# The keys of an RWKV mixer: two-part products in the dense projections, or exact float32 products among the scan's steps

## The chip, the cores and the metric

One core of a Trainium2 chip. The metric is the device time of one execution in microseconds (us). The kernel before was timed three times: 2986.07, 2990.43 and 2999.31 us; the median, 2990.43, stands for it.

## The reference

A stack of four layers of a model with 1024 features, batch 1: a short convolution and an attention layer (with feed-forward and mixture of experts) on 256 tokens, then two layers on 256 latent and 256 context tokens. The last layer's mixer is RWKV, and the change lies in it alone. Cut to what matters:

```python
def rwkv_project(h, shifted, mu, w_rkv, w0, w1, w2, a0, a1, a2, g1, g2, kvec):
    xx = shifted - h
    xr, xw, xk, xv, xa, xg = (h + xx * mu[i] for i in range(6))
    r = xr @ w_rkv[0]
    k = xk @ w_rkv[1]
    v = xv @ w_rkv[2]
    ...
    kk = to_heads(k * kvec[0], RW_HEADS).astype(jnp.float32)
    kk = kk / jnp.maximum(jnp.sqrt(jnp.sum(kk * kk, axis=-1, keepdims=True)), 1e-12)
    k = k * (1 + (a - 1) * kvec[1])

def rwkv7_scan(r, w, k, v, kk, a, S):
    def step(S, inp):
        rt, wt, kt, vt, kkt, at = inp
        sa = jnp.einsum("bhvk,bhk->bhv", S, -kkt)
        S = S * wt[:, :, None, :] + sa[..., None] * (kkt * at)[:, :, None, :] + vt[..., None] * kt[:, :, None, :]
        return S, jnp.einsum("bhvk,bhk->bhv", S, rt)
```

The keys `k` are one product: 512 tokens (context and latent) by 1024 features, with a 1024x1024 weight. Everything is float32.

## The kernel before

**Two ways to multiply float32.** Most dense products are made of two parts in the type float32r: `wchunk` (L254, L255) loads a 512 KB chunk of weights, ScalarE copies it into a high part `whi`, VectorE subtracts that to get the low part `wlo`; the other operand is split in the same way, and three products (high x high, high x low, low x high) are summed. `gemmN` (its products are L293) does this for features on partitions, a pair of 128-column blocks at a time. An exact product of plain float32 operands is one instruction in the program and two rows (passes) in the trace.

**Projections, `rwkv_project`.** `mix(i)` makes one of the six mixes of h and its shift, block by block of 128 features, and splits it into `mh` and `ml` (9 buffers each). First come the values V (L1591), 192 products of 128x512. Then `lowrank` (L1576) makes the first halves of the decay (`th`, 24 products of 128x512), of the in-context rate (`am`, 24 of 64x512), and of the gate (`gm`, 24 of 128x256). The keys' operand `kS` is left as plain float32: eight VectorE instructions, after `am`. The receptance's operand `rS` is made likewise. The residual x is then spilled to memory (`xd`, 1 MB), since its tile is used for the keys' weights and results.

**Scan, `rwkv_scan`.** The 1024 features are eight blocks of 128 (two heads each); a block b and a sequence s (0 context, 1 latent) are a unit, 16 in all. Each unit has stages, written as Python generators: `early` (decays, normalised keys kk, operands of the chunks; kk's last instruction is L1784), `inverse1`, `inverse2` (L1945 with the operand XX), `start_rh`, `chain` (four chunks of 64 tokens; L2015, L2022, L2027, L2038, L2045), `finish` and `finish2` (head norm, bonus, gate: L2078, L2095, L2097, L2103). A scheduler at the end of `rwkv_scan` takes, time and again, the generator with the earliest due time (the table PACE, in halves of a block's period) and runs it up to its next yield; so the order of instructions on every engine is fixed when the program is built. `receptance` (L1733) is one more generator at the start, and `project_a` to `project_7` make the output projection at the end.

**Keys in the scan.** `key_pieces` makes a block's keys in 16 exact products of 128x256 (L1698), each a piece of its own, into a PSUM bank named `kc`, and a ScalarE copy (L1703) into the second half of x's tile; the weights come in four DMAs of 128 KB into its first half. The pieces are drawn in order: 16 by a generator `k0` and 32 by `k1` at the scan's start, and 80 in the chains: by the table KP each chunk of units 0 to 9 issues one piece ahead of L2027 and one ahead of L2038:

```python
    KP = ((0, 1, 1),) * 10 + ((0, 0, 0),) * 6
    K0T = ((0.0, 0.02), (0.3, 0.08))
    NDS = ((0, 0, 0),) * 10 + ((2, 3, 3),) * 5 + ((0, 0, 0),)
...
        gens.append([K0T[0][0], K0T[0][1], keys(16, 1), "k0", []])
        gens.append([K0T[1][0], K0T[1][1], keys(32, 3), "k1", ["k0"]])
```

The first `early` waits for `k0`, the second block's for `k1`. By the table NDS the chains of units 10 to 14 issue products of zeros instead (L1994, bf16: 2, 3 and 3 for each chunk), which fill the array between small products.

Of the kernel before, what the change touches and what calls it, by code (L numbers as in the profile page):

```python
# [10 lines left out]
I32 = mybir.dt.int32  # L11
# [21 lines left out]
def _body(es, tc, A, out, upto, dbg):  # L33
# [10 lines left out]
    class Psum:  # L44
        def tile(self, shape, dtype, name, bufs=None, tag=None):
            tag = tag or name
            tag = sizes.get(tag) if isinstance(sizes.get(tag), str) else tag     # one tag may stand for another
            return self.pool.tile(shape, dtype, name=name, tag=tag, bufs=sizes.get(tag, 1))
# [3 lines left out]
    def phase(nm, banks, raw=4, hl=3, work=True, t2=6, sq2=2):  # L52
        """buffers of a phase: psum banks by tag, streamed weights, small temporaries"""
# [37 lines left out]
    def columns(name, parts):  # L91
        """parts: list of (key, AP [n,128]) with at most 128 rows; loads them -> function that gives {key: [128, n]}"""
# [35 lines left out]
    # silu(c) in zeros, to be placed at any column of 32; and silu(c_2), silu(c_ctx_2) side by side  # L128
# [4 lines left out]
    # [p, m]: 1 where p % 32 == m  # L133
# [6 lines left out]
    back.update(jobs=[], rate=0.0, credit=0.0)  # L140

    def back_step():
        """one step of the first job; clean: it holds no buffer now"""
        while back["jobs"]:
            try:
                back["clean"] = next(back["jobs"][0])
                return
            except StopIteration:
                back["jobs"].pop(0)

    def background(jobs, chunks):
        """add jobs (steps, generator), to be done within so many chunks"""
# [9 lines left out]
    def mods(name, W, n0, ncols, strip, nv, bcols):  # L162
        """W [1024, N]: columns n0..n0+ncols of silu(c) @ W + b -> one [128, ncols/128] per vector, (steps, generator)
        strip 0: for c; 1: for c_2 (and c_ctx_2). Four column groups of the array share the blocks of 128 rows;
        each run of 512 columns has its rows (one per vector) among the 32 of a group"""
# [32 lines left out]
    def mods_v(name, W, n0, ncols, vecs, bcols):  # L198
        """the same by VectorE: the sums over blocks of 128 rows, then over partitions"""
# [39 lines left out]
    def wchunk(ap, shape):  # L239
        """ap (or a list of APs side by side in the last dim), [128, a, b] with a * b <= 1024"""  # L240
# [17 lines left out]
    def gemmA(W, cols, xh, xl, emit, kmax=4):  # L258
        """feature-major: for each list of 128-column blocks (pairs) emit(pair index, psum [128,2,256])
        cols: list of lists of column starts handled in one chunk (2 blocks each)"""  # L260
# [15 lines left out]
    def gemmN(W, cols, xs, emit):  # L276
        """feature-major; xs: (hi, lo) [128, n] per block of features; emit(block, psum [128, n])"""
# [26 lines left out]
    lnw = const.tile([P, 1], F32, name="lnw")  # L304

    def warm_ln(after):
        """have the logarithm's table loaded once `after` is there, ahead of a norm"""
# [4 lines left out]
    class Stats:  # L312
        """sum over features of x^2, block by block of 128 as x comes to be; rstd: 1/sqrt(mean + eps), the same in all 128 rows.
        vec: VectorE adds the blocks up, else TensorE"""
# [40 lines left out]
    def modulated(pl, x, a, b, tag="h", bufs=3, st=None):  # L355
        """rms-normalised x times column a plus column b, in two parts"""
# [15 lines left out]
    def rstd2(x):  # L372
        """for x [128, 8, 2, 256]"""
# [5 lines left out]
    def scale_col(name, g, s):  # L379
        """g * (1 + s)"""  # L380
# [4 lines left out]
    def load_T(src, x):  # L385
        """[256, 1024] -> x [128, 8, 256]; loads, -> function that transposes"""
# [16 lines left out]
    xj = act.tile([P, KT, 2, T], F32, name="xj")     # residual streams: context, latent  # L403
# [85 lines left out]
    def layer1_attn():  # L489
# [7 lines left out]
        # rope tables, tokens on partitions  # L497
# [25 lines left out]
        # additive masks [query, tile's keys]: query tile 0 sees keys 0..127, query tile 1 keys 0..255  # L523
# [19 lines left out]
        # a group's heads i, 5 + i, 10 + i have one softmax: the groups' weights by their sums make it so  # L543
# [5 lines left out]
        def scores(i):  # L549
            """scores, masked; exp of them less their maximum; over their sum"""  # L550
# [61 lines left out]
        # probabilities, transposed; outputs feature-major  # L612
        oh = fb.tile([P, 8, T], F32R, name="oh", tag="h", bufs=3)
        ol = fb.tile([P, 8, T], F32R, name="ol", tag="h", bufs=3)
        for b in range(8):
# [4 lines left out]
            for h in range(2 * b, min(2 * b + 2, NH)):  # L620
                r0 = 64 * (h % 2)
                pt = ps.tile([P, 512], F32, name="tr", bufs=2)
                # [keys 0..127 | q tile 0, q tile 1], [keys 128..255 | q tile 1]
# [47 lines left out]
    def layer1_moe():  # L671
# [22 lines left out]
        # tokens on partitions, two parts  # L694
# [36 lines left out]
        # place of each token among its expert's tokens  # L731
# [99 lines left out]
        # an expert with more than 128 tokens: its other tokens  # L831
# [11 lines left out]
    def columns2():  # L843
        """loads; -> function that makes the columns"""
# [36 lines left out]
    def masks0(pl):  # L881
        nonlocal capf, capb, glm, reset, mdir, ones8
        # masks over pairs of tokens in one 128-token tile, [s, t]
# [6 lines left out]
        # t - s within chunks of 64, s on partitions twice  # L890
# [6 lines left out]
        # 0 where a chunk of 64 starts (forwards, backwards)  # L897
# [5 lines left out]
        mdir = pl.tile([8, 2], F32, name="mdir")     # 1 for forward rows, 1 for backward rows  # L903
# [4 lines left out]
    # states handed from the context scans to the latent scans  # L908
# [1429 lines left out]
```

## Time and profile before

| | us |
|---|---|
| runs of the kernel before | 2986.07, 2990.43, 2999.31 |
| their median | 2990.43 |
| the profiled execution, its span (no other time is given for it) | 2995.0 |
| TensorE products busy | 2811.6 (94%) |
| TensorE weight loads busy | 2282.7 (76%) |
| VectorE busy | 2269.9 (76%) |
| ScalarE busy | 1739.7 (58%) |
| share of the span of TensorE in the chain that ended last | 42% |

The span is that of one profiled execution; times of rows count from its start. PE is TensorE and PEld its weight loads, DVE VectorE, ACT ScalarE, POOL GpSimd, SP SyncE, which issues the DMAs. The end of a product is modelled (products overlap), so the distance of two starts says what one costs, and its busy time is longer. The RWKV projections end at 2224.25 us, and the scan's last stages at about 2764; the last feed-forward layer follows.

### The profile page before, as it was taken

What the parts mean: (1) busy time and instruction counts of PE and PEld (TensorE: products, weight loads), DVE (VectorE), ACT (ScalarE), POOL (GpSimd) and SP (SyncE); (2) the same over time, 40 slices, a digit from 0 to 9 for tenths busy, and PEclk for the clock granted to TensorE, in tenths of its full rate; (3) what the DMA queues carried; (4) which work ended last, traced back from release to release, by engine and by line L of the source; (5) the groups of instructions that cost most, each with busy time, mean ns of one, the idle gap of its engine ahead of it and who ended that gap; (6) DMA issues with size and microseconds to landing.
All of it is one profiled execution on the core that took longest, in us unless ns stands there. A gap on an engine that the chain in (4) does not pass through costs nothing.

```text
span 2995.0 us, 50233 instructions
## 1 busy us (share of the span) xinstructions
PE 2811.6 (94%) x19237; PEld 2282.7 (76%) x19237; DVE 2269.9 (76%) x3945; ACT 1739.7 (58%) x2937; POOL 16.8 (1%) x96
## 2 busy tenths in 40 slices
PE   7999899899999999997989989999699999999899
PEld 4989876688877877875767768888477777667898
DVE  3989673799898988998556388768767887674787
ACT  3465443677776877775556444334447677555554
POOL 0000000000000000000000000000000000000000
PEclk9999999999999999998989989999899999999899
DMA  9979677799898999993211235554222111113454
GB/s 310 329 265 356 217 229 249 273 348 355 296 373 312 343 328 337 355 333 109 79 35 50 72 98 170 178 167 154 78 75 50 28 30 20 18 26 103 128 178 133
DMA packets 410413, 567.74 MB, mean 190 GB/s; under 512 B 79719, under 2 KB 241715, under 8 KB 410163
## 3 DMA queue, kind: packets, MB, share of 16 engines
q1 hardware_dynamic: 406976, 561.79, 55.8%
q8 instruction: 153, 2.51, 0.3%
q10 hardware_dynamic: 3187, 2.65, 0.3%
q14 instruction: 97, 0.79, 0.1%
HBM read 559.11 MB, written 5.24 MB: 188 GB/s over the span
## 4 chain that ended last, share of the span: by engine, by line
PE 42%; DVE 7%; ACT 4%; issue 1%; DMA 1%; SPq 0%; ACTq 0%; DVEq 0%
PE mm L293 19%; PE mm L958 3%; PE yp L1390 2%; PE mm L1591 1%; PE tr L1958 1%; PE kc L1698 1%; PE p L2015 1%; PE p L1994 1%; PE p L2038 1%; PE mm L1856 1%; PE p L2027 1%; PE mm L1879 1%; PE tr L1945 1%; PE sc L1267 1%; PE p L2022 0%
## 5 line engine op out<-in xcount | busy, mean ns | idle before, releaser
L254 ACT ACTIVATE whi<-raw 128x1024 fp32r<-128x1024 f32 (+3 forms) x868 | 875.5, 1018 | 579.3 <-PE mm L293 154.0
L255 DVE TENSOR_TENSOR wlo<-raw,whi 128x1024 fp32r<-128x1024 f32 (+3 forms) x868 | 1002.4, 1171 | 196.1 <-ACT whi L254 167.1
L794 PE MATMUL mm<-wlo,XH 128*128 128x512 f32 (+1 forms) x768 | 288.6, 378 | 6.6 <-DVE wlo L255 6.1
L293 PE MATMUL mm<-hh,whi 128*128 128x512 f32 (+1 forms) x800 | 280.4, 352 | 11.4 <-ACT hh L926 4.3
L794 PE MATMUL mm<-whi,XL 128*128 128x512 f32 (+1 forms) x768 | 289.2, 377 | 0.0
L794 PE MATMUL mm<-whi,XH 128*128 128x512 f32 (+1 forms) x768 | 287.5, 374 | 0.2 <-ACT whi L254 0.2
L293 PE MATMUL mm<-hh,wlo 128*128 128x512 f32 (+1 forms) x800 | 279.0, 349 | 4.6 <-DVE wlo L255 4.6
L293 PE MATMUL mm<-hl,whi 128*128 128x512 f32 (+1 forms) x800 | 279.0, 350 | 0.0
L213 DVE SCALAR_TENSOR_TENSOR macc<-raw,sc,macc 128x512 f32<-128x512 f32 x238 | 175.7, 748 | 29.6 <-DMA raw<-in_w_mod_dram 25.8
L293 PEld LDWEIGHTS mm<-hh,whi 128*128 128x128 f32 x800 | 155.5, 195 | 32.0 <-ACT hh L926 5.1
L293 PEld LDWEIGHTS mm<-hh,wlo 128*128 128x128 f32 x800 | 154.7, 194 | 23.9 <-DVE wlo L255 5.0
L794 PEld LDWEIGHTS mm<-wlo,XH 128*128 128x128 f32 x768 | 145.0, 189 | 36.2 <-DVE wlo L255 10.9
L293 PEld LDWEIGHTS mm<-hl,whi 128*128 128x128 f32 x800 | 154.9, 194 | 19.3 <-issue 1.3
L794 PEld LDWEIGHTS mm<-whi,XL 128*128 128x128 f32 x768 | 145.0, 189 | 24.4
L794 PEld LDWEIGHTS mm<-whi,XH 128*128 128x128 f32 x768 | 145.2, 189 | 24.2 <-ACT whi L254 0.6
L271 PE MATMUL mm<-hh,whi 128*128 128x256 f32 x544 | 153.8, 284 | 6.7 <-ACT hh L365 6.7
L271 PE MATMUL mm<-hl,whi 128*128 128x256 f32 x544 | 153.1, 282 | 0.0
L271 PE MATMUL mm<-hh,wlo 128*128 128x256 f32 x544 | 152.7, 281 | 0.0
L1340 DVE SCALAR_TENSOR_TENSOR fg<-mm,c_fcw,fg 128x189 f32<-128x189 f32 (+2 forms) x352 | 144.0, 427 | 4.6
L812 PE MATMUL mm<-whi,muh 128*128 128x512 f32 x352 | 138.2, 393 | 0.1
L812 PE MATMUL mm<-whi,mul 128*128 128x512 f32 x352 | 137.2, 390 | 0.0
L812 PE MATMUL mm<-wlo,muh 128*128 128x512 f32 x352 | 117.3, 393 | 0.3
(718 smaller groups left out, 5968.2 us busy)
## 6 DMA issues: line engine op xcount, KB each, us to landing
raw<-in_moe_w_down_dram SPq DMA_DIRECT2D x176, 512.0 KB
raw<-in_moe_w_gate_dram SPq DMA_DIRECT2D x160, 512.0 KB
raw<-in_moe_w_up_dram SPq DMA_DIRECT2D x160, 512.0 KB
raw<-in_ffn_w_up_dram SPq DMA_DIRECT2D x110, 512.0 KB
raw<-in_mod_w_dram SPq DMA_DIRECT2D x96, 512.0 KB
raw<-in_w_mod_dram SPq DMA_DIRECT2D x96, 512.0 KB
raw<-in_ffn_w_down_dram SPq DMA_DIRECT2D x62, 512.0 KB
raw<-in_ev_w_in_dram SPq DMA_DIRECT2D x28, 512.0 KB
```

The source lines that it names most:

```text
L213: nc.vector.scalar_tensor_tensor(acc, w[:, kk], v[:, k + kk:k + kk + 1], acc, op0=OP.mult, op1=OP.add)
L254: nc.scalar.activation(hi[:, :n], raw[:, :n], AF.Copy)
L255: nc.vector.tensor_tensor(lo[:, :n], raw[:, :n], R(hi[:, :n]), op=OP.subtract)
L271: nc.tensor.matmul(pt[:, b], w[:, k, b * P:(b + 1) * P], x[:, k0 + k], start=(k0 + k + b == 0 and j == 0), stop=(k0 + k == kt - 1 and j == ...
L293: nc.tensor.matmul(pts[b], w[:, k, b * P:(b + 1) * P], x_, start=(k0 + k + j == 0 and (b == 0 or N != T)), stop=(k0 + k == kt - 1 and j == ...
L794: nc.tensor.matmul(pt[:, :n], xx[:, k0 + k, i], w[:, k], start=(k0 + k == 0 and j == 0), stop=(k0 + k == 7 and j == 2))
L812: nc.tensor.matmul(py[q], xx[:, k0 + k], w[:, k, q * 512:(q + 1) * 512], start=(k0 + k == 0 and j == 0), stop=(k0 + k == FB - 1 and j == 2))
L958: nc.tensor.matmul(pts[i][:, :n], x_, w[:, k], start=(k0 + k + j == 0), stop=(k0 + k == 7 and j == 2))
L1267: nc.tensor.matmul(o, l, r, start=(n == 0), stop=(n == len(jobs) - 1), skip_group_check=True)
L1340: nc.vector.scalar_tensor_tensor(d4[:, ro, co], s4[:, ri, cin], tap(dy, dx), d4[:, ro, co], op0=MULT, op1=ADD)
L1390: nc.tensor.matmul(yk[k], w[:, 0, k * P:(k + 1) * P], u, start=(f + b + j == 0 and k % 2 == 0), stop=(f + b == FB - 1 and j == 2 and k % 2 ...
L1591: nc.tensor.matmul(pts[i], x_, w[:, k], start=(k0 + k + j == 0), stop=(k0 + k == 7 and j == 2))
```

## The change

The keys are made in `rwkv_project` by `gemmN`, in three float32r products for each pair of blocks, between the first and the second low-rank product. `kS` then holds the keys themselves, so everything of the keys in the scan goes: the generators `k0` and `k1` and what waited for them, the pieces in the chains with the table KP, the bank `kc` (`tr` has two banks instead), the copies, the loads of weights, and the spill of x and its reload in `project_a`. The mixes get 14 buffers in place of 9. NDS and PACE stay as they are.

```diff
-    KP = ((0, 1, 1),) * 10 + ((0, 0, 0),) * 6
-    K0T = ((0.0, 0.02), (0.3, 0.08))
...
-                hi = pl.tile([P, 2 * T], F32R, name="mh", bufs=9)[:, :n]
-                lo = pl.tile([P, 2 * T], F32R, name="ml", bufs=9)[:, :n]
+                hi = pl.tile([P, 2 * T], F32R, name="mh", bufs=14)[:, :n]
+                lo = pl.tile([P, 2 * T], F32R, name="ml", bufs=14)[:, :n]
...
+        kS = o["k"] = pr.tile([P, KT, 2, T], F32, name="kS")
+        gemmN(rkv[1], [c * 256 for c in range(4)], mix(2), lambda k, p: nc.scalar.activation(f2(kS[:, k]), p, AF.Copy))
...
-        kS = o["k"] = pr.tile([P, KT, 2, T], F32, name="kS")
-        for k in range(KT):
-            nc.vector.scalar_tensor_tensor(kS[:, k], xx[:, k], C6["mu"][:, 16 + k:17 + k], hf[:, k], op0=MULT, op1=ADD)
...
-        def key_weights(b):
...
-        def key_pieces(b):
...
-        def keys(n, to):
...
-                kb = KN[b]
+                kb = kS[:, b]
...
-            nc.vector.tensor_tensor(km[:, 1], av[:, s], KN[b][:, s], op=MULT)
+            nc.vector.tensor_tensor(km[:, 1], av[:, s], kS[:, b, s], op=MULT)
...
-            ND, NK = NDS[2 * b + s], KP[2 * b + s]
+            ND = NDS[2 * b + s]
...
-                for _ in keys(NK[1], b + 4):
-                    pass
...
-            nc.sync.dma_start(x, xd)
-            banks.extend(ps.tile([P, 2, T], F32, name=n) for n in ("tr", "kc"))
+            banks.extend(ps.tile([P, 2, T], F32, name="tr") for _ in range(2))
...
-        gens.append([K0T[0][0], K0T[0][1], keys(16, 1), "k0", []])
-        gens.append([K0T[1][0], K0T[1][1], keys(32, 3), "k1", ["k0"]])
...
-                xd = dr.tile([P, KT, T], F32, name="xd")
-                nc.sync.dma_start(xd, x)
-            with phase("rs", dict(mm=2, tr=1, kc=1, p1=2, p2=1, p3=1, st="mm"), work=False), ExitStack() as st2:
+            with phase("rs", dict(mm=2, tr=2, p1=2, p2=1, p3=1, st="mm"), work=False), ExitStack() as st2:
```

Lines of the changed kernel have other numbers (the ones after the projections are lower by 38 to 44). What TensorE is given at three places:

At the projections' tail, TensorE, the last products of the decay's first half and what follows (`tr` is the low-rank sum, `mm` that of `gemmN`). Before:

```order
L1576 MATMUL tr<-mh,whi 128x512
L1576 MATMUL tr<-ml,whi 128x512
L1576 MATMUL tr<-mh,wlo 128x512
L1576 MATMUL tr<-mh,whi 64x512
L1576 MATMUL tr<-ml,whi 64x512
```

and after the change:

```order
L1574 MATMUL tr<-mh,whi 128x512
L1574 MATMUL tr<-ml,whi 128x512
L1574 MATMUL tr<-mh,wlo 128x512
L293 MATMUL mm<-mh,whi 128x512
L293 MATMUL mm<-ml,whi 128x512
L293 MATMUL mm<-mh,wlo 128x512
```

The rate's first half (64x512) follows after 192 rows of L293.

At the scan's start, TensorE, from the last product of the gate's first half (`kc` is a key's sum, `p` receptance's, `mm` here the decay's and the rate's second halves). Before:

```order
L1576 MATMUL tr<-mh,wlo 128x256
L1698 MATMUL kc<-kS,xj 128x256 x10
L1733 MATMUL p_28061<-rxh,rRH 128x256
L1698 MATMUL kc<-kS,xj 128x256 x2
L1733 MATMUL p_28061<-rxl,rRH 128x256
L1698 MATMUL kc<-kS,xj 128x256 x4
L1757 MATMUL mm<-th,w2s_28040 128x512
L1733 MATMUL p_28061<-rxh,rXX 128x256
```

and after the change:

```order
L1574 MATMUL tr<-mh,wlo 128x256
L1943 MATMUL p_28851<-V,anti 128x128 x2
L1695 MATMUL p_28355<-rxh,rRH 128x256
L1719 MATMUL mm<-th,w2s_28334 128x512
L1695 MATMUL p_28355<-rxl,rRH 128x256
L1719 MATMUL mm<-th,w2s_28334 128x512
L1726 MATMUL mm<-am,a2s_28335 128x512
L1695 MATMUL p_28355<-rxh,rXX 128x256
```

The first block's keys no longer stand ahead of receptance, and the first block's decay and rate come among its first products.

In the chains, TensorE, a chunk beside which a head norm's second half runs (`Tc,XT` is the inverse's product, `RH,BT` the state's, `gm,g2s` the gate's, `XX,xj` one of another unit's inverse). Before:

```order
L2015 MATMUL p_30747<-RH,TY_29838 64x64 x8
L2022 MATMUL p_30758<-RH,id_28048 64x128 x2
L2095 MATMUL mm<-rk,blk_27995 128x256
L2097 MATMUL mm<-ident,V 128x128 x2
L1698 MATMUL kc<-kS,xj 128x256 x2
L2027 MATMUL p_30762<-Tc,XT 64x64 x4
L2103 MATMUL mm<-gm,g2s 128x256
L1698 MATMUL kc<-kS,xj 128x256 x3
L2038 MATMUL p_30758<-RH,BT 64x64
```

and after the change:

```order
L2051 MATMUL mm<-rk,blk_28289 128x256
L1975 MATMUL p_31640<-RH,TY_30752 64x64 x8
L1982 MATMUL p_31651<-RH,id_28342 64x128 x2
L2053 MATMUL mm<-ident,V 128x128 x2
L1985 MATMUL p_31654<-Tc,XT 64x64 x4
L2059 MATMUL mm<-gm,g2s 128x256
L1907 MATMUL tr<-XX,xj 64x64 x3
L1994 MATMUL p_31651<-RH,BT 64x64
```

The keys ahead of the inverse's and of the state's product are gone, and nothing stands in their place but three products of another unit's inverse.

## Rows read from the trace of the kernel before

**Rows 1.** Stretches: us, busy (instructions) of five engines, PEclk, DMA share, GB/s.
```profile
2203.20:2224.25 21.05, 18.62 (x74) 13.04 (x73) 20.11 (x44) 12.28 (x24) 2.30 (x11) 0.84 0.00 0
2224.25:2266.30 42.05, 38.66 (x246) 34.27 (x246) 24.29 (x59) 28.85 (x47) 1.03 (x6) 0.96 0.42 131
2266.30:2299.30 33.00, 31.97 (x227) 24.68 (x225) 22.68 (x65) 19.54 (x46) 0.14 (x1) 1.00 0.24 53
2299.30:2349.78 50.48, 47.17 (x666) 35.94 (x666) 41.83 (x115) 38.32 (x90) 0.63 (x4) 1.00 0.17 32
2349.78:2563.91 214.13, 208.38 (x3005) 156.11 (x3002) 174.86 (x468) 152.59 (x390) 2.53 (x16) 1.00 0.14 25
2563.91:2632.56 68.65, 66.47 (x811) 44.20 (x811) 46.99 (x125) 40.72 (x105) 0.63 (x4) 0.91 0.08 13
```
The five engines are PE, PEld, DVE, ACT and POOL.

**Rows 2.** The normalised removal key: ns min/median/max, first and last start.
```profile
L1784 DVE SCALAR_TENSOR_TENSOR kk<-xj,kv,kk x8: 736/752/753, 2253.6 to 2632.6; 128x512 f32<-128x512 f32 x8
```

**Rows 3.** Timeline of TensorE (start us, us): the third-last value product, the first low-rank one.
```profile
2202.52 0.39 PE L1591 MATMUL mm<-whi,mh 128*128 128x512 f32 x1
...
2203.20 0.39 PE L1576 MATMUL tr<-mh,whi 128*128 128x512 f32 x1
```

**Rows 4.** Groups, 1800 to 2700: busy, mean ns of one, idle before and releaser.
```profile
L255 DVE TENSOR_TENSOR wlo<-raw,whi 128x1024 fp32r<-128x1024 f32 x62 | 75.5, 1220 | 19.6 <-ACT whi L254 19.4
L254 ACT ACTIVATE whi<-raw 128x1024 fp32r<-128x1024 f32 x61 | 64.5, 1057 | 116.0 <-PE mm L293 84.1 <-PE mm L1591 8.9 <-DMA raw<-in_ffn_w_up_dram 7.9
```

**Rows 5.** Timeline of TensorE: receptance products, two others of that form between them.
```profile
2232.88 0.28 PE L1733 MATMUL p<-rxh,rRH 128*128 128x256 f32 x1
...
2233.24 0.28 PE L1733 MATMUL p<-rxh,rRH 128*128 128x256 f32 x1
```

**Rows 6.** Timeline of TensorE: a wait in the tail, and the scan's first keys.
```profile
2217.44 0.53 PE L1576 MATMUL tr<-ml,whi 128*128 128x256 f32 x1 [0.73 <-DVE ml L301]
...
2224.25 4.53 PE L1698 MATMUL kc<-kS,xj 128*128 128x256 f32 x20
```

**Rows 7.** Stretches, passes of L1698 alone: us, PE busy, PEld busy, PEclk, DMA share, GB/s.
```profile
2224.25:2266.30 42.05, 11.66 (x45) 8.31 (x46) 0.96 0.42 131
2266.30:2299.30 33.00, 18.11 (x70) 12.01 (x69) 1.00 0.24 53
2299.30:2349.78 50.48, 9.27 (x34) 5.89 (x34) 1.00 0.17 32
2349.78:2563.91 214.13, 32.14 (x108) 17.60 (x108) 1.00 0.14 25
```

**Rows 8.** The block without keys, products of zeros (L1994) alone, same columns.
```profile
2563.91:2632.56 68.65, 18.31 (x61) 5.04 (x61) 0.91 0.08 13
```

**Rows 9.** Timeline of TensorE in that block: three products of zeros and their successor.
```profile
2582.68 0.82 PE L1994 MATMUL p<-one,zero 128*128 128x512 bf16 x3
2583.43 0.48 PE L2015 MATMUL p<-RH,TY 128*64 128x64 f32 x8
```

**Rows 10.** Timeline of TensorE: a chunk with keys beside a head norm.
```profile
2452.11 0.45 PE L2027 MATMUL p<-Tc,XT 64*64 64x64 f32 x8
...
2453.03 1.46 PE L1698 MATMUL kc<-kS,xj 128*128 128x256 f32 x6
...
2455.33 0.45 PE L2038 MATMUL p<-RH,BT 128*64 128x64 f32 x6 [0.22 <-DVE RH L2033]
```

**Rows 11.** Timeline of TensorE: the like chunk after the last key.
```profile
2556.95 0.45 PE L2027 MATMUL p<-Tc,XT 64*64 64x64 f32 x8
...
2560.38 0.44 PE L1945 MATMUL tr<-XX,xj 64*64 64x64 f32 x6 [2.14 <-ACT XX L1932]
...
2562.29 0.69 PE L2038 MATMUL p<-RH,BT 128*64 128x64 f32 x6 [0.83 <-DVE RH L2033]
```

**Rows 12.** Stretches of lower granted clock in the block without keys, columns as rows 1.
```profile
2562.27:2572.51 10.24, 10.22 (x100) 7.12 (x102) 6.73 (x15) 5.16 (x17) 0.00 (x0) 0.50 0.00 0
2610.06:2613.47 3.41, 3.41 (x23) 2.48 (x17) 0.42 (x2) 0.93 (x3) 0.14 (x1) 0.50 0.19 46
```

More of the change, by code (lines that the diff above doesn't have):

```diff
@@ L1610, in rwkv_project, with rwkv_scan @@
         return o
-    def rwkv_scan(pl, dr, o, free, x, xd, g):
+    def rwkv_scan(pl, dr, o, free, x, g):
         V, th, am, kS, gm, rS = (o[k] for k in ("V", "th", "am", "k", "gm", "r"))
@@ L1680, in rwkv_scan @@
         late = []
-        KN = {}
-        Wk = A["rw_w_rkv_2"][0, 1]
-        kw = lambda k: x[:, k // 2, P * (k % 2):P * (k % 2) + P]
-        def key_weights(b):
-            for k in range(0, KT, 2):
-                nc.sync.dma_start(x[:, k // 2].rearrange("p (i n) -> p i n", i=2),
-                                  Wk[k * P:(k + 2) * P, b * P:(b + 1) * P].rearrange("(i p) n -> p i n", p=P))
-        def key_pieces(b):
-            key_weights(b)
-            pk = ps.tile([P, 2, T], F32, name="kc")
-            for k in range(KT):
-                for s in range(2):
-                    nc.tensor.matmul(pk[:, s], kw(k), kS[:, k, s], start=(k + s == 0), stop=(k == KT - 1 and s == 1), skip_group_check=True)
-                    if k < KT - 1 or s == 0:
-                        yield
-            KN[b] = x[:, 4 + 2 * (b % 2):6 + 2 * (b % 2)]
-            assert b < 2 or (b - 2, 1) in done, b
-            nc.scalar.activation(KN[b], pk, AF.Copy)
-            yield
-        pieces = itertools.chain(*(key_pieces(b) for b in range(8)))
-        count = [0]
-        def keys(n, to):
-            for _ in range(n):
-                if count[0] == 16 * to:
-                    break
-                count[0] += 1
-                next(pieces)
-                yield
         def receptance():
@@ L2009, in chain @@
                 last = c == 3 and lat
-                for _ in keys(NK[0], b + 4):
-                    pass
                 p1 = zeros("p1", ND[0]).rearrange("p (a z v) -> p a z v", a=2, z=2)
@@ L2022, in chain @@
                         nc.tensor.matmul(p3[hh(h)], id0, RH[:, :, c, hh(h)], start=(ND[2] == 0), stop=False, skip_group_check=True)
-                for _ in keys(NK[1], b + 4):
-                    pass
                 p2 = zeros("p2", ND[1])[:, 0:128].rearrange("p (z v) -> p z v", z=2)
@@ L2033, in chain @@
                         nc.vector.tensor_copy(RH[0:64, :, c, hh(h)], p2[hh(h)])
-                for _ in keys(NK[2], b + 4):
-                    pass
                 if not last:
@@ L2217, in rwkv_scan @@
                 t0, t1, n = LAST.get((b, i), PACE[i])
-                gens.append([2 * b + t0, (t1 - t0) / n, f(*args), (b, i), [(b, j) for j in after] + (["r"] if (b, i) == (0, 1) else ["k0"] if (b, i) == (0, 0) else ["k1"] if (b, i) in ((1, 0), (0, 8)) else [])])
+                gens.append([2 * b + t0, (t1 - t0) / n, f(*args), (b, i), [(b, j) for j in after] + (["r"] if (b, i) == (0, 1) else [])])
         for (t0, dt), f, i, after in zip(PROJ, (project_a, project_6, project_b, project_7), "abcd",
@@ L2253, in layer2_1 @@
                 nc.vector.tensor_tensor(g, m(2), NG2(1, 1), op=MULT)
-                rwkv_scan(pl, dr, o, xj[:, :, 0], x, xd, g)
+                rwkv_scan(pl, dr, o, xj[:, :, 0], x, g)
         with phase("f1", dict(mm=4, tr="mm", st="mm")), ExitStack() as st:
```

## The prediction

> **What bounds the kernel now.** I read the change's stretches first, then its instructions in them. The keys of the RWKV mixer touch two places: the end of the projections and the scan. In the table of stretches [rows 1] the projections' tail (2203.20 to 2224.25) keeps VectorE busy for 20.11 of 21.05 us and TensorE for 18.62, at a granted clock of 0.84. The scan begins with two stretches (75 us in all) in which receptance, keys and the first block run together. Then follow blocks of features, one each time that the removal key is normalised on VectorE, eight times between 2253.6 and 2632.6 [rows 2]; the stretches of that table from 2299.30 on end at such marks. Four blocks with keys take 214.13 us, 53.5 each; the first block without keys takes 68.65 [rows 1]. In the four, TensorE is busy for 208.38 us (97%) and its weight loads for 156.11 (73%). The reader is to see that this busy share alone doesn't decide the case: the end of a small product is modelled, and products fill places in which the chain waits for ScalarE and VectorE.
>
> **Part 1: products added to the projections.** gemmN issues 4 column pairs x 8 feature blocks x 2 halves x 3 parts = 192 products of 128x512. Three such products of the value stand 2203.20 - 2202.52 = 0.68 us apart [rows 3], so 0.227 each: 192 x 0.227 = **+43.5 us**. They stand on TensorE between the first and second low-rank product, with nothing beside them there, so all of it is on the path.
>
> What comes with them: eight weight chunks (8 DMAs of 512 KB, one for every 24 products, 5.4 us), each with a ScalarE copy of 1.06 us and a VectorE subtraction of 1.22 [rows 4]; eight copies and subtractions that split the mix, and eight copies out, on half as many columns. Even at the weights' price that is 3 x 8 x 1.06 = 25 us on ScalarE and 2 x 8 x 1.22 = 20 on VectorE, beside 43.5 us of products. I cost them at nothing; without that cover they would be 20 to 25 us. The eight operands of the keys were made on VectorE before too, and cancel. On SP's queue 32 loads of 128 KB, the spill of x and its reload go; eight 512 KB loads come in, queued before the low-rank weights. DMA share in the tail is 0.00 [rows 1], so no transfer is displaced.
>
> **Part 2: the tail gets cheaper.** It has 24 + 24 products on 512 columns and 24 on 256. The narrow ones stand 0.12 us apart, 0.36 for three [rows 5], so the array needs 48 x 0.227 + 24 x 0.12 = 13.8 us, against 21.05; the gaps are waits for the mix's low part, as 0.73 us in [rows 6]. Behind 43.5 us of keys VectorE can be ahead, as far as 14 buffers in place of 9 let it. Kept waits are 0 to 3 us; I take 1.3, so **-6** (-7 to -4).
>
> **Part 3: the keys leave the scan's start.** One key product is two passes of a 128x256 product; ten of them open the scan at 2224.25 as x20, busy 4.53 [rows 6]; less the 0.17 by which the last end overlaps, that is 0.218 a pass, 0.437 a product, and 56 us for all 128. The stretch to 2266.30 has 45 passes, the next 70 [rows 7], 9.8 and 15.3 us at that spacing. The second stretch can't shrink below VectorE's 22.68 us of 33.00 [rows 1], so at most 10.3 comes back there; the first has ScalarE at 28.85 of 42.05 and may give all 9.8. The ends are 0 (receptance waits for its weights' DMA and splits whatever TensorE does) and -20.1. No row is nearer to either; I take the middle, **-10** (0 to -20).
>
> **Part 4: the keys leave the chains.** There are 34 and 108 passes in the stretches from 2299.30 and from 2349.78 [rows 7], 7.4 and 23.5 us. If all came back a block would take 53.5 - 5.9 = 47.6. But what stands in a key's place once it is gone? The nearest row is the block that has no keys: 68.65 us, with 61 zero products that fill [rows 8]. In row time these are 18.31 us, which leaves 50.3; by their spacing (2583.43 - 2582.68 = 0.75 for three [rows 9], 0.25 each, 15.3) it leaves 53.4, the period with keys. After the change units 0 to 9 have neither keys nor fillers, so I take the middle of 50.3 and 53.5: -1.6 for each of four blocks, and -1.9 for the one before by its share of passes: **-8**.
>
> That little comes back shows where one step of the chain stands beside its like. With keys, from the inverse's product to the state's at the head norm: 2452.11 to 2455.33, 3.2 us, with three key products (1.46) inside [rows 10]. Without: 2556.95 to 2562.29, 5.3 us, of which 2.14 are TensorE idle behind ScalarE's XX and 0.83 behind RH [rows 11]. ScalarE's queue there holds the copy that the chain needs behind XX and the norm's functions; the product that waits is late by that, and everything behind it on TensorE's queue is too. The order of the changed kernel has the same sequence (inverse's product, gate's product, L1907 behind XX, state's product) in every block.
>
> TensorE's busy share of 97% says that array time is what each block costs. By that the chains would give back all 31; by the step just shown most of it stays. The Trainium skill ("Perfetto Trace Analysis", Identifying the Most-Contended Engine) says that the busy share of matmuls is no good measure of how near TensorE is to its limit and that the share of weight loads is a better one; that speaks for the second reading, and the trace, with 73% against 97% in the same four blocks, agrees.
>
> **The sum.** 43.5 - 6 - 10 - 8 = **+19.5** us. The profiled execution's span is 2995.0, so 3014.5 in its terms; the median of the runs is 4.6 lower, so **3010 us**. With part 3 from 0 to -20 and part 4 from 0 to -17 (a block of 50.3), the forecast's own case runs from 2991 to 3028.
>
> **The rivals.**
>
> *All array time returns (faster).* If TensorE is the bound wherever keys stand, their 56 us come off one for one against +37.5 in the projections: -18.5, so 2972. At the start that would need VectorE's work to move from the second stretch into the first, which is possible: the first block's early stage waits for the first keys now, and for nothing of theirs afterwards. For it: 97% busy [rows 1], the granted clock at 1.00, and VectorE at 174.86 and ScalarE at 152.59 of 214.13, both below the 190 that would be left. Against it: the idle 2.14 and 0.83 where no key stands. It decides only if nearly all returns, at a period of 48 us. Chance 0.15.
>
> *The clock falls in every block (much slower).* No key is left to keep the array filled. In the block after the last key the granted clock stood at 0.50, the lower level of 1.2 GHz, from 2562.27 for 10.24 us and once more for 3.41 [rows 12], although the block has fillers; while keys ran it was 1.00 in all four blocks [rows 1]. Just before the first fall came the waits of [rows 11]. Half of 10.24 us is lost each time, 5.1. If each of five periods keeps its length and takes one fall, 37.5 - 10 + 5 x 5.1 = +53, so 3043. Against it: the blocks in the middle have an early stage beside the chain that the last blocks lack. The Trainium skill ("TensorE: Matmul & The Clock Gate", HAM oscillation) says that pauses between bursts of products bring the clock down again for each burst; the trace shows it twice, both without keys. It decides at one fall in each block. Chance 0.17.
>
> *Covers only.* Periods stay as they are and the clock too: 37.5 - 10 = +27.5, 3018; that is the upper part of the forecast's case and no case of its own.
>
> **How the numbers follow.** A measurement of this kernel can tell 0.5% (15 us) from no change: 2975.5 to 3005.4. The forecast's case has 0.60, of which a third, 0.20, lies below 3005.4; all array time has 0.15, two thirds of it past the bound of faster; the clock has 0.17; the 0.08 that is left I put mostly near no change. So faster 0.11 (0.10 + 0.01), same 0.31 (0.20 + 0.05 + 0.06), slower 0.58 (0.40 + 0.17 + 0.01). For 8 in 10 the range runs from 2974, near the faster rival's time, to 3036, short of the slower one's.
>
> **What would show it.** In the changed kernel's profile: products of L293 with mh some 43 us long between the two low-rank ones, spaced 0.227; the tail after them near 15 us; the scan's two first stretches together near 65 us; marks of the normalised key (now L1746) 51 to 53 us apart, with TensorE's busy share in the blocks down to some 85%, and idle before it behind ScalarE's XX and RH. Marks 48 us apart would show the faster rival; a granted clock of 0.50 inside blocks 2 to 6, the slower one. The prediction is wrong at its root if the added products are not spaced at 0.227, or if weight chunks arrive late.

## The result, and the profile after

The changed kernel takes 3021.59 us (median of four runs, 3019.03 to 3024.21) against 2993.03 for the kernel before in the same sessions: a ratio of 1.0097, interval 1.0079 to 1.0114, slower by 28.6 us. The profiled execution's span grew from 2995.0 to 3020.6, 25.6 us. Forecast were 3010 us and 19.5 us more.

The stretches of the changed kernel, with the columns of [rows 1] (us, busy and instructions of PE, PEld, DVE, ACT and POOL, PEclk, DMA share, GB/s). The first holds as many products as were added, 192: 24 of the decay and 168 of the keys. Then come the last 24 of the keys with the rest of the projections, the scan's start up to the second mark of the normalised key, one block, four blocks, one block.

```profile
2204.33:2247.90 43.57, 43.57 (x194) 36.09 (x193) 24.29 (x31) 19.65 (x30) 0.00 (x0) 1.00 0.22 67
2247.90:2261.78 13.88, 13.88 (x73) 10.50 (x71) 10.46 (x31) 7.04 (x14) 1.45 (x7) 1.00 0.12 37
2261.78:2332.12 70.34, 51.48 (x371) 41.78 (x372) 49.72 (x127) 51.32 (x98) 1.88 (x11) 0.85 0.25 71
2332.12:2383.57 51.45, 44.19 (x635) 34.04 (x631) 39.98 (x111) 33.19 (x81) 0.63 (x4) 0.88 0.12 19
2383.57:2592.49 208.92, 192.53 (x2842) 146.12 (x2842) 169.65 (x458) 147.76 (x377) 2.54 (x16) 0.97 0.12 19
2592.49:2661.69 69.20, 64.22 (x834) 44.05 (x843) 51.10 (x136) 43.65 (x113) 0.64 (x4) 0.95 0.09 13
```

[Rows 1] are cut at another place near the start; these are two stretches of the kernel before that end at the marks, and answer to the third and fourth above.

```profile
2224.25:2303.81 79.56, 75.12 (x545) 62.79 (x545) 50.14 (x128) 52.84 (x98) 1.18 (x7) 0.98 0.33 94
2303.81:2349.78 45.97, 42.69 (x594) 32.10 (x592) 38.66 (x110) 33.87 (x85) 0.63 (x4) 1.00 0.16 29
```

Read as a ledger against [rows 1]: the projections from the last value product on take 43.57 + 13.88 = 57.45 us in place of 21.05, **+36.4**, with TensorE busy all the time. The start takes 70.34 in place of 79.56, **-9.2**. The block behind it takes 51.45 in place of 45.97, **+5.5**; the two together, which does not hang on the mark between them, -3.7. The four blocks that held 54 of the keys' products take 208.92 in place of 214.13, **-5.2**, the block after them 69.20 in place of 68.65. With -2.1 in the last stages of the scan this is 25.9, the span's 25.6.

So the array gave up 23.5 us of keys in the four blocks, and 5.2 came back. TensorE's idle time there is 208.92 - 192.53 = 16.4 us where it was 214.13 - 208.38 = 5.8, so 10.6 became waiting. The mean clock of 0.97 says that some 13 us ran at half speed, which takes another 6 to 7, where TensorE is busy. In the block before them the clock of 0.88 stands for as much, 12 to 13 us at half speed, where the kernel before had 1.00. What TensorE waits for in the four blocks (us in total, times, longest), changed kernel, waits of 2383.57 to 2592.49:

```profile
PE tr L1907 <- ACT XX L1894: 7.1, 5, 2.8
PE p L1994 <- ACT RH L1989: 3.1, 7, 1.3
PE p L1994 <- DVE RH L1991: 1.4, 4, 0.8
```

The chunk of [rows 10], at the same place of the changed kernel's timeline of TensorE:

```profile
2483.02 0.45 PE L1985 MATMUL p<-Tc,XT 64*64 64x64 f32 x8
2483.40 0.70 PE L2059 MATMUL mm<-gm,g2s 128*128 128x256 f32 x2
2485.44 0.33 PE L1994 MATMUL p<-RH,BT 128*64 128x64 f32 x2 [1.35 <-ACT RH L1989]
...
2486.27 0.28 PE L1994 MATMUL p<-RH,BT 128*64 128x64 f32 x2 [0.25 <-DVE RH L1991]
```

From the inverse's product to the state's second part it is 3.25 us, where it was 3.22 with three key products inside. The state's first product, which waits for ScalarE's copy RH, stands 2.42 us behind the inverse's; in the kernel before (at 2454.41) it stood 2.30 behind, and the gate's and the key products filled that time.

In the start the granted clock was low, and there was a long wait: two stretches (columns as above), and a row of the timeline.

```profile
2307.38:2317.62 10.24, 9.05 (x32) 6.85 (x31) 7.77 (x24) 2.55 (x8) 0.00 (x0) 0.50 0.06 6
2324.44:2338.10 13.66, 5.33 (x91) 5.08 (x92) 12.91 (x34) 12.22 (x28) 0.14 (x1) 0.50 0.16 22
```

```profile
2331.40 0.48 PE L1907 MATMUL tr<-XX,xj 64*64 64x64 f32 x4 [9.15 <-ACT XX L1894]
```

In the first stretch TensorE is busy for 9.05 of 10.24 us at half clock. In the second it waits: for 9.15 us it has nothing to do until the first inverse's blocks come from VectorE and ScalarE, which are busy for 12.91 and 12.22 of the 13.66 us around it.

### The profile page after: what moved, and what is told of

Its sections match the earlier page's. It is cut to its first block, busy times and chain, and to the rows that moved or that the text cites. A ratio compares the mean times of both kernels' runs of the same rounds, so it can differ in the third digit from the quotient of the medians.

```text
span 3020.6 us, 50107 instructions
## 1 busy us (share of the span) xinstructions
PE 2802.8 (93%) x19150; PEld 2283.1 (76%) x19173; DVE 2284.0 (76%) x3961; ACT 1753.7 (58%) x2953; POOL 16.6 (1%) x96
## 4 chain that ended last, share of the span: by engine, by line
PE 41%; DVE 6%; ACT 4%; DMA 1%; issue 1%; ACTq 0%; SPq 0%; DVEq 0%
PE mm L293 21%; PE mm L958 3%; PE yp L1390 2%; PE mm L1589 1%; PE tr L1920 1%; PE p L1975 1%; PE p L1956 1%; PE p L1994 1%; PE mm L1818 1%; PE p L1695 1%; PE sc L1267 1%; PE tr L2103 1%; PE tr L1907 1%; PE p L1985 0%; PE tr L1574 0%
## 5 line engine op out<-in xcount | busy, mean ns | idle before, releaser
L254 ACT ACTIVATE whi<-raw 128x1024 fp32r<-128x1024 f32 (+2 forms) x876 | 884.1, 1019 | 581.9 <-PE mm L293 164.6
L255 DVE TENSOR_TENSOR wlo<-raw,whi 128x1024 fp32r<-128x1024 f32 (+2 forms) x876 | 1012.6, 1172 | 207.9 <-ACT whi L254 180.1
L293 PE MATMUL mm<-hh,whi 128*128 128x512 f32 (+1 forms) x800 | 279.9, 352 | 11.8 <-ACT hh L926 4.3
L293 PE MATMUL mm<-hh,wlo 128*128 128x512 f32 (+1 forms) x800 | 278.4, 349 | 4.6 <-DVE wlo L255 4.6
L293 PE MATMUL mm<-hl,whi 128*128 128x512 f32 (+1 forms) x800 | 278.5, 349 | 0.1
L293 PEld LDWEIGHTS mm<-hh,whi 128*128 128x128 f32 x800 | 154.8, 194 | 32.4 <-ACT hh L926 5.1
L293 PEld LDWEIGHTS mm<-hh,wlo 128*128 128x128 f32 x800 | 154.2, 193 | 24.0 <-DVE wlo L255 5.0
L293 PEld LDWEIGHTS mm<-hl,whi 128*128 128x128 f32 x800 | 154.5, 193 | 19.4 <-issue 1.3
```

The lines of the kernel that those rows point to most:

```text
L254: nc.scalar.activation(hi[:, :n], raw[:, :n], AF.Copy)
L255: nc.vector.tensor_tensor(lo[:, :n], raw[:, :n], R(hi[:, :n]), op=OP.subtract)
L293: nc.tensor.matmul(pts[b], w[:, k, b * P:(b + 1) * P], x_, start=(k0 + k + j == 0 and (b == 0 or N != T)), stop=(k0 + k == kt - 1 and j == ...
```

## The experiments

Two theories went in. **Waits**: the scan is paced by ScalarE and VectorE, the keys filled gaps, and their array time is worth nothing once gone. **Clock**: the array time would come back, but without keys TensorE falls to the lower clock and gives it away again. A third, **array**, is that each product costs what it takes. Times are medians beside the kernel before on the same chip, 2991 to 2993; the changed kernel stands at 3021.6.

### 1 and 2. Products of zeros ahead of the chain's own sums

```diff
-    NDS = ((0, 0, 0),) * 10 + ((2, 3, 3),) * 5 + ((0, 0, 0),)
+    NDS = ((0, 1, 1),) * 10 + ((2, 3, 3),) * 5 + ((0, 0, 0),)
```

> The changed kernel, with one product of zeros ahead of the inverse's and one ahead of the state's sum in each chunk of units 0 to 9, about where the keys stood (80 products of 0.22 to 0.25 us, some 19 us of array time). Covers (what the keys filled were waits for ScalarE and VectorE, so the chain's pace is set by those engines): the time stays within 5 us of the changed kernel's 3021.6, and the blocks' marks stay 49 to 54 us apart. Clock (the keys' array time did come back, and the spells at 0.50 between 2307 and 2601, 51 us in all, ate it): the spells shrink to less than half, and the time falls by 10 to 20 us, to 3002 to 3012. Array bound: slower by up to 19 us.

With 2, 3 and 3 for the first fifteen units:

> The changed kernel, with the last blocks' products of zeros (2, 3 and 3 a chunk) in units 0 to 9 too: 320 products, some 75 us of array time, more than the keys' 31 in the chains. Covers: the waits of a chunk hold about as much as the keys took, so the rest, some 40 us, comes on top: 3050 to 3065. Clock: the granted clock is 1.00 from the first chain to the last key's place, which gives back 25 us, and the rest costs some 40: 3035. If it is faster than the changed kernel, neither holds and the clock is worth more than the spells show.

The light filling took 3033.32 us (1.0139, 1.0119 to 1.0158), 11.7 more than the changed kernel: neither waits nor clock, but the array's case. The full one took 3061.03 (1.0223, 1.0207 to 1.0240), as waits had it and not the clock. This filling did not help. But these products write into the bank of the sum that follows, so they can only start once that bank is read: they stand in the chain, where the keys, in a bank of their own, did not.

### 3. The changed kernel without the dense products

```diff
-        gemmN(rkv[1], [c * 256 for c in range(4)], mix(2), lambda k, p: nc.scalar.activation(f2(kS[:, k]), p, AF.Copy))
+        for k in range(KT):
+            nc.vector.scalar_tensor_tensor(kS[:, k], xx[:, k], C6["mu"][:, 16 + k:17 + k], hf[:, k], op0=MULT, op1=ADD)
```

> The changed kernel without the 192 dense products of the keys, their weights, splits and copies; the scan then takes the keys' operand for the keys, so the keys are left out of the computation. If the change is worth what its two stretches show (projections +36.4, scan -10.6), this is 36 us below the changed kernel, 2985, and 8 to 11 below the kernel before. If the added stage moves anything else (weights of later stages, the clock at the scan's start), it lies more than 5 us off that.

2984.69 us (0.9966, 0.9952 to 0.9980): 36.9 below the changed kernel. That this is near the ledger's +36.4 is chance, since the ledger compares with the longer tail of the kernel before. In the profiles the stage is 57.45 - 14.35 = 43.1 us shorter, all that the dense products take; the scan up to its last mark is 3.4 longer, and what lies behind the mark 6.3, which was not explained. Even with all keys left out of the program, only some 8 us come off the kernel before, most of them in the projections' tail, which is short although no dense products stand ahead of it:

```profile
2201.67:2216.02 14.35, 14.27 (x73) 10.71 (x71) 13.13 (x31) 8.51 (x19) 2.30 (x11) 1.00 0.00 0
```

### 4. The kernel before without keys in the chains

```diff
-    KP = ((0, 1, 1),) * 10 + ((0, 0, 0),) * 6
+    KP = ((0, 0, 0),) * 16
...
+        for b in range(3, 8):
+            KN[b] = x[:, 4 + 2 * (b % 2):6 + 2 * (b % 2)]
```

> The kernel before with the 80 key products in the chains taken out, and with them the weights and copies of blocks 3 to 7, which use the keys of blocks 1 and 2 (so those keys are left out of the computation). Projections and the scan's start as before. Covers: the chains keep their pace and the time stays within 5 us of the kernel before, 2988 to 2998. Array bound: 31 us less, 2962. Clock: the time stays as well, or falls by under 8, and the granted clock falls to 0.50 inside the blocks from 2303 to 2560, where it stood at 1.00.

3003.37 us (1.0033, 1.0009 to 1.0057): **80 products less, and slower**. No theory had this. The granted clock fell as the clock theory said, but that cost more than the missing products gave. Even the fastest execution is only 3.5 us below the kernel before, for 35 us of products less. Twelve runs of this one program spread from 2989.72 us at a mean granted clock of 0.962 to 3025.96 at 0.948. The profiled one (span 3020.6) shows where, in the four blocks:

```profile
2353.17:2586.97 233.80, 217.68 (x2824) 168.57 (x2823) 171.45 (x458) 148.74 (x376) 2.54 (x16) 0.83 0.11 17
```

A mean clock of 0.83 where it was 1.00 [rows 1], PE busy 217.68 for less work, and the stretch 19.7 us longer.

### 5. Zeros in the keys' bank, half as long

```diff
+            if b > 2:
+                pk = ps.tile([P, 512], F32, name="kc")
+                for i in range(16):
+                    nc.tensor.matmul(pk, zero, one, start=(i == 0), stop=(i == 15), skip_group_check=True)
+                    yield
+                return
             key_weights(b)
```

> The kernel before, with each of the 80 key products in the chains replaced by one bf16 product of zeros of 128x512 into the keys' own bank (some 0.22 us in place of 0.44); blocks 3 to 7 use the keys of blocks 1 and 2, so their keys are left out of the computation. Without any product there the time was 3003 (2990 to 3026), with the granted clock at 0.50 inside the blocks. Clock (the keys' worth in the chains is that they keep the array busy, so the clock up): the zeros hold the clock near 1.00 in blocks 2 to 6, half of the array time comes back, and the time is 2980 to 2988, narrowly spread. Waits (products at those places only fill what ScalarE and VectorE leave): the clock too may hold, but the time is that of the kernel before, 2990 to 2997. If half as much work does not hold the clock: 2995 to 3010, as without keys.

2996.40 us (1.0011, 1.0000 to 1.0022), from 2990.98 to 3001.59: the waits' case. Four blocks in the profile:

```profile
2348.69:2562.38 213.69, 198.65 (x2888) 147.45 (x2888) 174.85 (x469) 151.00 (x383) 2.54 (x16) 0.97 0.12 19
```

PE is busy 9.7 us less, and the stretch is as long as with keys (214.13). But the zeros do not stand at the keys' places. All of them had run early in the scan, while the last key of the kernel before starts at 2542.4:

```profile
L1699 PE MATMUL kc<-one,zero x80: 376/379/390, 2290.8 to 2398.8; 128*128 128x512 bf16 x80
```

So the last three of the four blocks have neither keys nor zeros. These three in experiment 5, in the kernel before and in experiment 4:

```profile
2401.51:2562.38 160.87, 146.23 (x2153) 110.57 (x2152) 130.81 (x349) 113.10 (x287) 1.91 (x12) 0.96 0.12 19
2403.29:2563.91 160.62, 155.85 (x2232) 116.46 (x2232) 131.20 (x351) 113.91 (x291) 1.90 (x12) 0.99 0.13 24
2408.01:2586.97 178.96, 166.11 (x2130) 128.61 (x2132) 130.12 (x349) 113.50 (x287) 1.91 (x12) 0.82 0.11 17
```

The kernel before has 40 keys there, 17.4 us. With all of them gone the stretch is as long: TensorE's idle time grew from 4.8 to 14.6 us, and the clock, 0.96 in place of 0.99, takes some 5. **What the keys filled was, for the larger part, waiting.** Experiment 4 has no product there either, but ran at 0.82 and took 18 us more, with less idle time (12.9 us): what it lost, it lost to the clock. Why the clock held in the one and fell in the other these runs do not show.

### 6 and 9. The same in the changed kernel, and its bank alone

Experiment 6 has 128 such products, for all the keys, and takes the inverse's second bank for them; experiment 9 takes the bank and leaves it empty.

```diff
-            with phase("rs", dict(mm=2, tr=2, p1=2, p2=1, p3=1, st="mm"), work=False), ExitStack() as st2:
+            with phase("rs", dict(mm=2, tr=1, kc=1, p1=2, p2=1, p3=1, st="mm"), work=False), ExitStack() as st2:
```

> The changed kernel with 128 such products of zeros where the 128 key products stood, at the start and in the chains, in a bank of their own, taken from the second bank of the inverse's sums as in the kernel before. They wait for no bank, which the products of zeros ahead of the chain's own sums did (3033). Clock: spells at 0.50 in the scan fall from some 54 us to under 20, and the time falls by 8 to 18 us, to 3004 to 3014. Waits: within 5 us of 3021.6. Array: slower by up to 28 us, 3050.

> The changed kernel with one bank for the inverse's sums in the scan, as before the change, the other left empty until the output projection. With products of zeros in that bank the time was 3026.4 (granted clock mean 0.963), with the second bank 3021.6 (0.958). Waits and clock together (without products at the keys' places and with one bank the chains lose their pace, as in the kernel before without chain keys, 3003 against 2993): 3030 to 3045, clock at or below 0.955. Waits alone: 3021 to 3027, since neither the zeros nor the bank matter. If it is below 3020, the second bank did harm.

With zeros 3026.44 us (1.0115, 1.0096 to 1.0134), with the empty bank 3025.00 (1.0106, 1.0084 to 1.0129): neither is told apart from the changed kernel. The clock theory forecast 3004 to 3014, but this is no test of it in the blocks: the zeros had all run by 2422.1, 113 of the 128 ahead of the third mark, and in the four blocks the clock was 0.95.

Up to the third mark experiment 6 took 122.5 us at a clock of 0.97; the changed kernel took 70.34 + 51.45 = 121.8 at 0.85 and 0.88. Experiment 9, with the same banks and no zeros, took 116.7 at 0.87. So of some 25 us of added products 6 show there. Whether the rest filled waits or the higher clock paid for it is not separated.

The four blocks of experiment 9 (its profiled execution took 3029.12 us):

```profile
2374.49:2599.76 225.27, 209.84 (x2824) 160.69 (x2823) 171.47 (x457) 148.61 (x376) 2.54 (x16) 0.85 0.11 18
```

They are 16 us longer than in the changed kernel, at a clock of 0.85 in place of 0.97, while the stretch up to the third mark is 5.1 shorter. So without products in the blocks the clock fell in the two profiles with one bank for the inverse's sums (experiments 4 and 9), and stood at 0.95 to 0.97 in the three with two (the changed kernel, 3 and 8). That is one execution of each.

### 7 and 8. The buffers of the mixes alone

```diff
-                hi = pl.tile([P, 2 * T], F32R, name="mh", bufs=9)[:, :n]
-                lo = pl.tile([P, 2 * T], F32R, name="ml", bufs=9)[:, :n]
+                hi = pl.tile([P, 2 * T], F32R, name="mh", bufs=14)[:, :n]
+                lo = pl.tile([P, 2 * T], F32R, name="ml", bufs=14)[:, :n]
```

> The kernel before with 14 buffers for the mixes in place of 9, nothing else. The projections' tail took 21.05 us before; without the dense keys but with 14 buffers it took 14.46. If the buffers gave that (and not the cover of the dense products): tail 14 to 15 us, time 5 to 7 us below the kernel before, 2987. If not: the tail stays at 21 and the time within 2 us.

The reverse, in the changed kernel:

> The changed kernel with 9 buffers for the mixes in place of 14. If the buffers gave the short tail: the stretch from the last value product to the last low-rank one grows from 57.5 to 64 us or more (the keys' mix can't be split ahead either), and the time to 3027 to 3033. If the dense products' cover gave it: within 2 us of 3021.6.

The kernel before with 14 buffers takes 2988.37 us (0.9986, 0.9973 to 0.9999). Its tail:

```profile
2198.32:2212.67 14.35, 14.28 (x74) 10.76 (x73) 13.14 (x31) 8.51 (x19) 2.31 (x11) 1.00 0.00 0
```

The buffers alone shorten the tail by 6.7 us. With 9 the changed kernel's stage (the dense products and the tail) takes 60.31 us, 2.9 longer than with 14, less than was expected, and its time, 3024.05 (1.0107, 1.0089 to 1.0126), is not told apart: the dense products cover part of the same wait.

### 10. More at the keys' places

```diff
+                    if b > 2 and k + s > 0 and k + s < KT:
+                        nc.tensor.matmul(f2(pk), zero, one, start=False, stop=False, skip_group_check=True)
```

> The kernel before, with a bf16 product of zeros of 128x512 added into the sum behind 70 of the 80 key products in the chains (some 0.22 us each, 15.4 in all; the keys are unchanged). At those places nothing gave 3003, 0.22 us gave 2996, the keys' 0.44 gave 2993. Waits: there is room for some more, the time stays within 5 us of the kernel before. Array: the places are full at 0.44, and all 15 us come on top: 3008.

3002.99 us (1.0035, 1.0023 to 1.0046), 10 us slower: between the two, nearer to the array's 15. The four blocks:

```profile
2350.69:2582.89 232.20, 229.75 (x3056) 165.88 (x3055) 176.51 (x470) 153.43 (x390) 2.53 (x16) 1.00 0.13 24
```

TensorE is busy 229.75 of 232.20 us, at a clock of 1.00, and the stretch is 18.1 us longer. 53 of the 70 added products lie in it, and five more of the keys than before, some 14 us of array time in all. The block behind it takes 60.5 in place of 68.7, at a clock of 1.00 in place of 0.91, which gives some back. So the series is: nothing in the chains 3003, 80 zeros of 0.22 us (all early) 2996, the keys' 0.44 us 2993, 0.66 us 3003. **Products in the chains are free up to about the keys' length; beyond it they cost in full in those blocks.** With keys the clock of the four blocks was 1.00, without any product between 0.83 and 0.97.

### 11. Better filling in the blocks after the keys

```diff
-    KP = ((0, 1, 1),) * 10 + ((0, 0, 0),) * 6
-    NDS = ((0, 0, 0),) * 10 + ((2, 3, 3),) * 5 + ((0, 0, 0),)
+    KP = ((0, 1, 1),) * 10 + ((0, 2, 2),) * 4 + ((0, 0, 0),) * 2
+    NDS = ((0, 0, 0),) * 14 + ((2, 3, 3),) + ((0, 0, 0),)
...
+            if to > 8:
+                pk = ps.tile([P, 512], F32, name="kc") if n else None
+                for i in range(n):
+                    nc.tensor.matmul(pk, zero, one, start=(i == 0), stop=(i == n - 1), skip_group_check=True)
+                    yield
+                return
```

> The kernel before with 14 buffers for the mixes (2988), and in units 10 to 13 the products of zeros that stand ahead of the chain's own sums (2, 3 and 3 a chunk) replaced by 2 and 2 a chunk in the keys' bank, at the keys' places: 64 in place of 128. If products in a bank that nobody waits for fill without delaying the chain, the block that took 68.7 us takes 58 to 63, and the time is 2975 to 2982. If they only have to hold the clock, and half as many don't, spells at 0.50 grow in those two blocks and the time is 2988 to 2995.

**2975.14 us** (0.9940, 0.9924 to 0.9955), 18 below the kernel before and the best of all. The first block without keys took 68.24 us in experiment 7, with 65.98 of busy TensorE, 61 products of zeros and a clock of 0.92. Here it has 28 of them:

```profile
2550.10:2603.63 53.53, 52.33 (x723) 36.06 (x722) 43.91 (x118) 37.74 (x95) 0.63 (x4) 1.00 0.11 17
```

That is 14.7 us less, with 13.7 less of busy TensorE, and a clock that stays at 1.00. This run does not separate the number of the products from their bank and place; experiment 12 bears on it.

### 12. The changed kernel with the same filling

The table KP and NDS of experiment 11, its products of zeros for all units, and the banks of experiment 9.

> The changed kernel with one bank for the inverse's sums and the other for products of zeros at the keys' old places: 1 and 1 a chunk in units 0 to 9, 2 and 2 in units 10 to 13 in place of 2, 3 and 3 ahead of the chain's own sums; none at the scan's start. The same stages then stand with the keys dense (this) and in the scan (2975). Waits: the chains have the same pace in both, the start is 9 us shorter here, the projections 43 longer: 2975 + 43 - 9 = 3009. If the keys' array time in the chains were worth anything beside zeros of half that time, 17 us come off that: 2992. If the clock in the first stretches of the scan, which nothing holds here, costs time: 3015 to 3020.

3011.03 us (1.0064, 1.0046 to 1.0082), 2 us from the waits' sum. With the same table of filling on both sides the dense keys are 36 us slower than keys in the scan. The filling ran at other places, though: its products in the bank `kc` all start by 2542.8. So the block that has 28 in experiment 11 has no product of zeros at all here:

```profile
2592.02:2648.74 56.72, 51.57 (x724) 39.21 (x722) 44.01 (x118) 38.83 (x100) 0.63 (x4) 0.86 0.10 16
```

It takes 56.7 us, at the lower clock, against 68.2 with 61 zeros in the banks of the chain's own sums and 53.5 with 28 in a bank of their own. So what made the block short is above all that those 61 were gone.

## Why the prediction was right

The sign, the mechanism and most terms held; the size was 9 us short.

- **Added products, +43.5.** Right: 57.45 us for 264 products, without a wait, and 43.1 us less of that stage without them (experiment 3). ScalarE (26.69) and VectorE (34.75) fit under them, as costed.
- **The tail, -6.** Without the 43.57 us of the added products 13.88 are left of 21.05, -7.2, with no kept waits. The reason was half right: 14 buffers alone do it (experiment 7), and the cover of the dense products was not needed.
- **The scan's start, -10.** It measured -9.2 up to the second mark.
- **The block behind the start, -1.9.** This is the step that failed: +5.5, and with the start -3.7 for a forecast of -11.9. The sum scaled this block from the four behind it (by passes that is -2.0) and had no term for the clock, which it kept for a rival. The block ran 12 to 13 us at half speed, which takes up to 6 to 7 us, and TensorE's idle time grew from 3.3 to 7.3. What made the clock fall is open. With two banks for the inverse's sums (the changed kernel, experiments 1, 3 and 8) this block took 49.4 to 53.0 us at a mean clock below 1.00; with one bank and a clock of 1.00 it took 46.0 to 48.9. Experiment 9, with one bank, took 47.9 at a low clock, and experiment 4 53.0. So bank and clock are not told apart as the cause.
- **The four blocks, -6.4.** They gave -5.2. The mechanism was right for the larger part: 10.6 us became waiting, behind XX and RH as was said. That the size came out is luck. It was the middle of two ends with no reason for the middle; it left out the lower clock, which took 6 to 7; TensorE was busy for 92%, not 85; and one end, 50.3, was read from the wrong row: the block with products of zeros is no chain without keys, since those zeros made it longer than no filling does (experiment 12). Without keys or zeros three blocks take 53.6 us each at 0.96, the period with keys (experiment 5).
- **The last stages.** They gave -2.1, for which the forecast had no term.
- **The rivals.** All array time returning is refuted for the chains: 40 keys out of three blocks return nothing (experiment 5), and all out of the chains cost 10 us (experiment 4). The clock rival, 3043, came about by half: it had one fall of 10.24 us in each of five periods, and the first of them ran 13 us at the lower clock, the other four some 13 together. In the profile of experiment 4, whose slowest run is at 3026, the clock of 0.83 stands for some 80 us at half speed in the four blocks alone. "Covers only", +27.5, which I folded into the forecast, was the nearest number, +28.6, but its condition, that periods and clock stay as they are, did not hold.

What TensorE's busy share told (97% in the four blocks) was not that array time is what they cost. The Trainium skill ("Perfetto Trace Analysis", Identifying the Most-Contended Engine) says that the busy share of matmuls is no good measure of how near TensorE is to its limit. The runs agree, with 9.7 us less of busy TensorE and 0.4 us less of time in the four blocks of experiment 5. But from there up the share was to be taken at its word: experiment 10 put some 14 us of products into the four blocks and got 18 us more.

## What to carry to other kernels

Before moving work from a loop that is bound by waits to a dense stage, ask what the work costs where it stands: take it out, or put in half or twice as much, and look in the trace where the products stand that you put in. Here 35 us of products in the chains gave nothing back when they were taken out, since waits for ScalarE and VectorE, and a lower clock, took their place. 43 us in a dense stage are paid in full, even at a lower cost for each product. In a bank that nothing in the chain waits for, 28 products of zeros did no harm (a block of experiment 11). In the banks of the chain's own sums 80 products cost 11.7 us (experiment 1), and the block after the keys was longer with its 61 than with none (experiment 12).

## What was not expected

Taking work off TensorE made the kernel slower and its time uncertain: one program without keys in the chains ran from 2989.72 us (mean granted clock 0.962) to 3025.96 (0.948), while the kernel before stayed within 2986 to 3001 in the same session. The profile (span 3020.6) shows the clock at 0.83 in the four blocks; what makes it fall in one execution and not in the next was not found. Nor did the products of zeros stay where the program has them: those of experiments 5, 6 and 12 ran far ahead of the keys' places, while the keys themselves, and what was added behind them in experiment 10, were spread over the blocks.
